# A Winograd-style 3x3 convolution on one core: the weights in transfers of 116 and 12 partitions, one store less finely cut, and two images' loads taken apart

## The chip, the cores and the metric

The kernel runs on one core of a Trainium2 chip. The time is the device time of one execution in microseconds (us). Durations of single steps come from one profiled execution, whose times are counted from the start of its span.

## The reference

A 3x3 convolution with padding 1, 16 images of 64 x 64 pixels with 64 channels in and 128 out, all float32:

```python
batch, c_in, h, w, c_out = 16, 64, 64, 64, 128
x_pad = np.pad(x, ((0, 0), (0, 0), (1, 1), (1, 1)), mode='constant')
output[b, co] += weight[co, ci, kh, kw] * x_pad[b, ci, kh:kh+h, kw:kw+w]   # summed over ci, kh, kw
```

## The kernel before

Two images form a pair: the 64 channels of one lie on partitions 0 to 63, those of the other on 64 to 127. There are eight pairs (0 to 7), and each is worked off in two halves of 32 output rows (the loop that starts at line 218). GpSimd (POOL) forms the sums and differences of input rows that the algorithm needs (`sums`, `diffs`, `outers`, lines 110 to 128; those of the first half are done by VectorE, DVE), ScalarE (ACT) makes a 16-bit copy of some rows (`cast`), TensorE (PE) multiplies by transformed weights (line 170), and ACT and DVE add the results up into output tiles (lines 192 and 247 to 253).

Before that the weights have to be made ready: `w_raw`, 128 rows of 2304 bytes, is loaded (line 59), turned into 16 bits by POOL (line 87) and ACT (line 88), transposed by nine matmuls (line 102), and combined into `Wt` by ACT and DVE (lines 139 to 150). Ahead of its first instruction of line 88 ACT loads its function table, which the compiler places there.

All transfers are issued by SyncE (SP) in the order in which they are written; a wait of one holds up those behind it. SP issues, in this order: the weights; the first pair in two parts (rows 0 to 33 and 34 to 63, called x0a and x0b below); pairs 1 and 2; pairs 3 and 4 in one transfer into the tile `two` (line 81); then the store of pair 0, and from there on stores as pairs are done, with the loads of pairs 5, 6 and 7 among them as their places come free. The pairs 0, 3 and 6 are stored by one transfer of two images (line 207), the others by one for each image (line 216). The second image of pair 5 is an exception: rows 0 to 56 go out in one transfer, and its last seven rows in a transfer of 124 partitions and one of 4:

```python
parts = [(0, CO, 0, H)]
if (p, b2) == FEW[:2]:                 # FEW = 5, 1, 7
    at = H - FEW[2]
    parts = [(0, CO, 0, at), (0, 124, at, H), (124, 4, at, H)]
```

A transfer is cut into packets, one for each contiguous run of a partition (16384 bytes for a whole image of one channel), and these are spread over the rings of up to 16 DMA engines, which work through them in order. The stores are named o0 to o7 here, with a and b for a pair's first and second image where each has its own, and the loads x0a, x0b, x1, x2, x34, x5, x6, x7.

Of the kernel before, what the change touches and what calls it, by code (L numbers as in the profile page):

```python
# [15 lines left out]
def kernel(  # L16
# [12 lines left out]
    nc = tc.nc  # L29
    B, CI, H, W = x.shape  # L30
    CO = weight.shape[0]
# [4 lines left out]
    keep = tc.keep_in_program_order  # L36
    x_rows = x.rearrange("b c h w -> (b c) h w")
    w_flat = weight.rearrange("co ci kh kw -> co (ci kh kw)")
# [10 lines left out]
    X_HOME = [0, 1, 2, ("d", 0), ("d", 1), 2, ("d", 0), ("d", 1)]  # L49
    O_HOME = ["b", (3, 4), (0, 1), "b", (3, 4), (0, 1), "b", (2, 3)]  # L50
    BOTH = (0, 3, 6)
    FEW = 5, 1, 7
    NEXT_LOADS = {(1, 1): 5, (3, 0): 6, (4, 0): 7}

    def home(k, name):
        return slots.tile([128, H, W], F32, tag=f"s{k}", name=name)

    w_raw = const.tile([CO, CI * 9], F32)
    keep(nc.sync.dma_start(w_raw, w_flat))
    xs = {}  # L60

    def load(p, cuts=((0, H),)):
        if X_HOME[p] in range(5):
            xs[p] = home(X_HOME[p], "xs")
        for lo, hi in cuts:
            keep(
                nc.sync.dma_start(
                    xs[p][:, lo:hi, :], x_rows[128 * p : 128 * p + 128, lo:hi, :]
                )
            )  # L70

    two = slots.tile([128, 2, H, W], F32, tag="d", name="two")
# [4 lines left out]
    load(0, ((0, 34), (34, H)))  # L77
    load(1)
    load(2)
    rows = x_rows[128 * 3 : 128 * 5, :, :].rearrange("(g p) h w -> p g h w", g=2)  # L80
    keep(nc.sync.dma_start(two, rows))

    ident = const.tile([128, 128], F16)
    make_identity(nc, ident)
# [113 lines left out]
    def outputs(p):  # L198
        if O_HOME[p] == "b":
            both = slots.tile([128, 2, H, W], F32, tag="b", name="both")  # L200
            return both, [both[:, b2, :, :] for b2 in range(2)]
        return None, [home(k, "ot") for k in O_HOME[p]]

    def store(p, both, ots):
        if p in BOTH:
            pair = out[2 * p : 2 * p + 2, :, :, :].rearrange("b c h w -> c b h w")
            keep(nc.sync.dma_start(pair, both))
            return
        for b2 in range(2):
            parts = [(0, CO, 0, H)]  # L210
            if (p, b2) == FEW[:2]:
                at = H - FEW[2]
                parts = [(0, CO, 0, at), (0, 124, at, H), (124, 4, at, H)]
            for c, n, lo, hi in parts:
                keep(
                    nc.sync.dma_start(
                        out[2 * p + b2, c : c + n, lo:hi, :], ots[b2][c : c + n, lo:hi, :]
                    )
                )

    for n, (p, h) in enumerate(halves):
        if n + 2 < len(halves):
            tr[halves[n + 2]] = transforms(nc.gpsimd, *halves[n + 2])
        if h == 0:
            both, ots = outputs(p)
# [28 lines left out]
        if h == 1:  # L254
            store(p, both, ots)
# [32 lines left out]
```

## Time and profile before

| | us |
|---|---|
| median of 3 runs (lowest to highest) | 127.10 (126.88 to 127.14) |
| the profiled execution's own time | 127.13 |
| its span | 125.4 |
| PE busy / POOL busy / ACT busy / DVE busy | 95.6 / 90.5 / 85.4 / 66.8 |
| bytes moved by DMA, mean rate | 50.78 MB, 405 GB/s over the span |
| last DMA packet of the span | ends at 124.17 |

The profiled execution lies 0.03 us above the median. Of its 127.13 us, 1.73 lie outside the span, and 1.18 inside it after the last packet. The page's busy shares are means over the whole span; its second part cuts the span into 40 slices of 3.1 us, a digit of 9 meaning 90% busy or more.

### The profile page before, as it was taken

To read this page: it belongs to the slowest core of one execution; us is meant where nothing else is said; L and a number is where in the kernel's file an instruction comes from. 1 tells how busy PE (TensorE), PEld (TensorE's weight loads), DVE (VectorE), ACT (ScalarE), POOL (GpSimd) and SP (SyncE) were. 2 spreads that over 40 slices of the span, in tenths; PEclk is the share of its full clock that TensorE was granted. 3 is DMA by queue.
4 is the path that set the end of the run, shared out by engine and by line. 5 is a ranking of instruction groups with operands and counts; after the bars stand their busy time and mean duration, and the time that the engine had idled before them with its cause. 6 is when DMAs were issued, how large, how long until landed. Compare 5 with 4: busy or idle time off the path is not lost.

```text
span 125.4 us, 2343 instructions
## 1 busy us (share of the span) xinstructions
PE 95.6 (76%) x873; PEld 48.9 (39%) x873; DVE 66.8 (53%) x104; ACT 85.4 (68%) x150; POOL 90.5 (72%) x52
## 2 busy tenths in 40 slices
PE   0349999999999999999999999999999960000000
PEld 0223555555455555555555555555555520000000
DVE  0199658393939476574939394765749390000000
ACT  4458598989797988989897979789898930000000
POOL 2209999999999999999999999999999300000000
PEclk9999999999999999999999999999999996555555
DMA  4999999999999999999999999999999999999971
GB/s 132 371 453 423 434 424 439 423 335 418 434 431 429 426 434 418 423 429 434 416 439 424 423 423 423 418 431 434 423 424 423 433 416 443 423 429 444 418 335 47
DMA packets 3827, 50.78 MB, mean 405 GB/s; under 512 B 360, under 2 KB 488, under 8 KB 744
## 3 DMA queue, kind: packets, MB, share of 16 engines
q1 hardware_dynamic: 3816, 50.63, 96.2%
q8 instruction: 7, 0.11, 0.3%
q14 instruction: 4, 0.03, 0.1%
HBM read 17.07 MB, written 33.55 MB: 404 GB/s over the span
## 4 chain that ended last, share of the span: by engine, by line
PE 76%; DMA 2%; DVE 2%; POOL 1%; DVEq 0%; ACT 0%; issue 0%
PE acc L170 75%; DMA w_raw<-in_weight_dram 2%; DVE ss L114 1%; DVE ot L251 1%; POOL w L87 1%; DVEq L283 0%; DVE th L141 0%; DVE Wt L142 0%; PE wp L102 0%; ACT g0h L139 0%; DVEq L142 0%
## 5 line engine op out<-in xcount | busy, mean ns | idle before, releaser
L170 PEld LDWEIGHTS <-Wt 64*128 64x128 f16 x864 | 48.0, 96 | 48.5 <-issue 3.0
L192 ACT COPY ut<-acc 128x512 f32<-128x512 f32 x96 | 48.7, 612 | 4.4 <-PE acc L170 4.4
L170 PE MATMUL acc<-xh,Wt 64*128 64x504 f16 (+3 forms) x384 | 46.2, 372 | 0.0
L170 PE MATMUL acc<-ss,Wt 64*128 64x504 f16 (+1 forms) x192 | 24.8, 392 | 2.3 <-DVE ss L114 2.3
L170 PE MATMUL acc<-ee,Wt 64*128 64x504 f16 (+1 forms) x192 | 26.4, 377 | 0.0
L247 DVE TENSOR_TENSOR ot<-acc,ut 128x512 f32<-128x512 f32 x20 | 12.9, 686 | 20.0 <-ACT ut L192 15.8
L114 POOL TENSOR_TENSOR ss<-xs 128x1024 f16<-128x1024 f32 x7 | 16.6, 2366 | 4.7 <-DMA xs<-in_x_dram 4.7
L127 POOL TENSOR_TENSOR ee<-two 128x1024 f16<-128x1024 f32 x8 | 19.0, 2378 | 0.0
L114 POOL TENSOR_TENSOR ss<-two 128x1024 f16<-128x1024 f32 x8 | 19.0, 2369 | 0.0
L127 POOL TENSOR_TENSOR ee<-xs 128x1024 f16<-128x1024 f32 x7 | 16.6, 2376 | 0.0
L253 ACT COPY ot<-acc 128x512 f32<-128x512 f32 x20 | 10.7, 589 | 5.5 <-PE acc L170 5.5
L170 PE MATMUL acc<-dd,Wt 64*128 64x504 f16 (+1 forms) x96 | 13.9, 392 | 0.0
L247 DVE TENSOR_TENSOR both<-acc,ut 128x512 f32<-128x512 f32 x12 | 7.7, 686 | 11.0 <-ACT ut L192 7.9
L251 DVE TENSOR_TENSOR ot<-ut,acc 128x512 f32<-128x512 f32 x20 | 12.8, 682 | 0.2
L249 DVE TENSOR_TENSOR ot<-acc,ut 128x512 f32<-128x512 f32 x20 | 12.8, 680 | 0.0
L121 POOL TENSOR_TENSOR dd<-two 128x512 f16<-128x512 f32 x8 | 10.3, 1287 | 0.0
L121 POOL TENSOR_TENSOR dd<-xs 128x512 f16<-128x512 f32 x7 | 10.0, 1423 | 0.0
L132 ACT CAST xh<-two 128x1088 f16<-128x1088 f32 x8 | 9.3, 1157 | 0.0
L132 ACT CAST xh<-xs 128x1088 f16<-128x1088 f32 x8 | 9.2, 1145 | 0.0
L253 ACT COPY both<-acc 128x512 f32<-128x512 f32 x12 | 6.4, 589 | 3.5 <-PE acc L170 3.5
L251 DVE TENSOR_TENSOR both<-ut,acc 128x512 f32<-128x512 f32 x12 | 7.7, 683 | 0.1
L249 DVE TENSOR_TENSOR both<-acc,ut 128x512 f32<-128x512 f32 x12 | 7.7, 680 | 0.0
(23 smaller groups left out, 14.9 us busy)
## 6 DMA issues: line engine op xcount, KB each, us to landing
out_dram<-ot SPq DMA_DIRECT2D x9, 2048.0 KB, 18.5
out_dram<-both SPq DMA_DIRECT2D x3, 4096.0 KB, 22.5
xs<-in_x_dram SPq DMA_DIRECT2D x3, 2048.0 KB, 16.2
two<-in_x_dram SPq DMA_DIRECT2D x1, 4096.0 KB, 28.4
two<-in_x_dram SPq DMA_DIRECT2D x2, 2048.0 KB, 23.1
out_dram<-ot SPq DMA_DIRECT2D x1, 1824.0 KB, 24.3
xs<-in_x_dram SPq DMA_DIRECT2D x1, 1088.0 KB, 5.4
xs<-in_x_dram SPq DMA_DIRECT2D x1, 960.0 KB, 7.4
```

What stands on the lines that cost most here:

```text
L87: keep(nc.gpsimd.tensor_copy(w16[:, 0, :], w_raw))
L114: keep(eng.tensor_add(t, v[:, j : j + 16, 0, :], v[:, j : j + 16, 1, :]))
L121: keep(eng.tensor_sub(t, v[:, j : j + RB, 1, :], v[:, j : j + RB, 0, :]))
L127: keep(eng.tensor_sub(t, xs[p][:, r - 1 : r + 15, :], xs[p][:, r + 1 : r + 17, :]))
L132: keep(nc.scalar.copy(t, xs[p][:, C_ROW[h] : C_ROW[h] + 17, :]))
L170: nc.tensor.matmul(tiles[b2][:, lo:hi, c_lo:c_hi], Wt[p0 : p0 + 64, wi, kw, :], src[p0 : p0 + 64, first : last + 1 : step, c_lo + kw - 1 : ...
L192: keep(nc.scalar.copy(ut, tiles[b2]))
L247: keep(nc.vector.tensor_add(ov[b2][:, jg : jg + RB, 1, :], pg2[b2], ug[b2]))
L249: keep(nc.vector.tensor_add(ov[b2][:, jf : jf + RB, 0, :], pf1[b2], uy[b2]))
L251: keep(nc.vector.tensor_sub(ov[b2][:, jf : jf + RB, 1, :], ux[b2], pf2[b2]))
L253: keep(nc.scalar.copy(ov[b2][:, jg : jg + RB, 0, :], pg1[b2]))
```

## The change

Three edits. The weights come in two transfers, of partitions 0 to 115 and 116 to 127. Pairs 3 and 4 are loaded by a transfer each. The second image of pair 5 is stored by one transfer of 128 partitions, as the other single images are. The number of transfers stays at 24.

```diff
-    FEW = 5, 1, 7
+    FEW = 116
...
-    keep(nc.sync.dma_start(w_raw, w_flat))
+    for c in (slice(0, FEW), slice(FEW, CO)):
+        keep(nc.sync.dma_start(w_raw[c, :], w_flat[c, :]))
...
-    rows = x_rows[128 * 3 : 128 * 5, :, :].rearrange("(g p) h w -> p g h w", g=2)
-    keep(nc.sync.dma_start(two, rows))
+    load(3)
+    load(4)
...
         for b2 in range(2):
-            parts = [(0, CO, 0, H)]
-            if (p, b2) == FEW[:2]:
-                at = H - FEW[2]
-                parts = [(0, CO, 0, at), (0, 124, at, H), (124, 4, at, H)]
-            for c, n, lo, hi in parts:
-                keep(
-                    nc.sync.dma_start(
-                        out[2 * p + b2, c : c + n, lo:hi, :], ots[b2][c : c + n, lo:hi, :]
-                    )
-                )
+            keep(nc.sync.dma_start(out[2 * p + b2, :, :, :], ots[b2]))
```

## The prediction, made before the result was known

> **What bounds the kernel now.** The page's slices come first: they show which resource is never idle.
>
> ```profile
> PE   0349999999999999999999999999999960000000
> ...
> DMA  4999999999999999999999999999999999999971
> GB/s 132 371 453 423 434 424 439 423 335 418 434 431 429 426 434 418 423 429 434 416 439 424 423 423 423 418 431 434 423 424 423 433 416 443 423 429 444 418 335 47
> ```
>
> The DMA engines are full from the second slice to the 38th of 40; PE stops in the 33rd. The windows view of the end says the same:
>
> ```profile
> 28.40:100.00 71.60, 71.60 (x676) 36.78 (x672) 45.51 (x74) 63.69 (x114) 69.88 (x36) 1.00 1.01 426
> 100.00:119.40 19.40, 2.41 (x24) 0.98 (x18) 3.68 (x6) 1.44 (x3) 0.00 (x0) 0.62 1.01 430
> 119.40:124.20 4.80, 0.00 (x0) 0.00 (x0) 0.00 (x0) 0.00 (x0) 0.00 (x0) 0.50 0.51 218
> ```
>
> The share before the last figure is the DMA's: full to 119.4, half in the last 4.8 us, where rings finish one after the other. So the end is set by the last of 16 rings, and the page's chain, which ends in PE, misleads: PE only hands over stores, and those wait behind others.
>
> The trace also keeps every DMA packet with start, duration and bytes, without its ring. In steady state a packet starts 2 to 4 ns before the one ahead of it ends, so I strung the packets into 16 rings by fitting starts to ends and sizes to the issue order (in the first 3 us the fit is ambiguous). A 16384-byte packet takes 611 ns, 607 from start to start. Rings end between 120.18 and 124.17. Four facts matter. (1) The 128 packets of 1792 bytes (124 + 4 partitions) lie on four rings, 32 on each; these end at 122.60, 122.91, 123.20 and 123.38. (2) One ring, the slow ring, has stores of 644 ns in the median against 611; it ends at 124.07 and is none of the four. (3) The last, the late ring, ends at 124.17; it lost some 0.6 us to an instruction packet of 16 KB at 21.3 us and then 2.8 us to slow loads (the last two packets of x34, the last three of x6); it is none of the four either. (4) The other ten end at 122.62 or sooner.
>
> The start comes next: the chain in order of time, then SP and ACT in the timeline.
>
> ```profile
> 0.74 2.95 DMA w_raw<-in_weight_dram
> ...
> 3.74 0.67 POOL w L87
> ...
> 8.00 94.44 PE acc L170 x864
> ```
>
> ```profile
> 0.74 0.38 SPq L59 DMA_DIRECT2D w_raw<-in_weight_dram  x1
> 1.18 0.42 SPq L67 DMA_DIRECT2D xs<-in_x_dram  x1
> 34.14 0.36 SPq L216 DMA_DIRECT2D out_dram<-ot  x1
> 80.76 0.33 SPq L216 DMA_DIRECT2D out_dram<-ot  x1
> 81.15 1.67 SPq L216 DMA_DIRECT2D out_dram<-ot  x2
> 0.73 1.28 ACT L88 ACT_TABLE_LOAD   x1 [0.73 <-PEq L272]
> 3.71 0.67 ACT L88 CAST w<-w_raw 128x576 f16<-128x576 f32 x1 [1.70 <-DMA w_raw<-in_weight_dram]
> ```
>
> PE runs 94.44 us without a pause, so what it loses at the start it never regains. The fifth SP row is the pair of 124 and 4 partitions: 0.78 and 0.83 us of issue by the trace, where whole transfers of 128 partitions that wait for nothing take 0.33 to 0.45.
>
> **The store of pair 5.** The other twelve rings, slow and late one among them, get 16384 bytes a row instead of 14592: 8 rows x 66 ns (607 less 541) = +0.53 us; on the slow ring, 5% slower, +0.56. The four rings lose 32 packets of 70 ns (2.24 us) and gain 0.53: -1.71. Two transfers and their 1.6 us of issue go; that costs or saves nothing, as the next store waits until 92.3 us for its data.
>
> **The weights on the rings.** From fact (1), 124 went to four rings of 31 and 4 to four of 1, so 116 goes to four rings with 29 packets. For 12 no row shows whether three or one a ring. (By the Trainium skill, "DMA: Bandwidth & Descriptors", section "Why a DMA increments its semaphore by 16 and not by 1", the count is the largest divisor up to 16, so twelve rings; no run here shows it.) At 90 ns a packet after the first, the four rings get 21 or more on top of their 8, +2.0 us, against -1.71 from the store: +0.3, ending at 123.7. They stay behind the slow and the late ring.
>
> **The start of the loads.** Twelve rings lose 7 or 8 weight packets; the weights occupy them from 1.74-2.30 to 2.8-3.3, then x0a starts at 2.79-3.29. But x0a is now issued third. Two bounds. If the new issues take what the old one took (0.38), x0a is issued at 1.60; with the 1.01 to 1.56 that the weights needed from issue to first packet it starts at 2.6-3.16: -0.15. If they cost what 124 and 4 partitions cost (0.78 and 0.83, and two gaps of 0.05), x0a is issued at 2.45 and starts at 3.46-4.0: +0.7. Below the first bound a gain needs the slow first x0a packets (0.34 us of excess a ring) to vanish too. I take +0.7: these rows are the nearest, also transfers over few rings, and their waits (transfers ended 10 us before) can't fill the time. (The Trainium skill, same page, "Issuing engines are not separate DMA queues", says the time to initiate a DMA is usually small relative to the DMA itself; the pair's 1.67 us contradicts it here. By it the sum would come out as in the first rival.)
>
> **The weights' way to PE.** The four rings finish 29 packets, with the first one's 0.3 us, at about 4.8, and the 12 partitions at 4.9, against 3.3. In the built program ACT's table load, which waited for nothing, now waits for the 12 partitions. So 1.28 us that lay beside the transfer comes behind it: ACT's copy ends near 5.3 + 1.28 + 0.67 = 7.3 instead of 4.4, and PE starts about 2.9 us late. Every store is handed over 2.9 us late. Cover: the tightest is o1a, issued at 34.14 and reached by the first ring at 37.92, 3.8 us of which an issue needs up to 1.56. It becomes ready at 38.0-38.6; most rings, moved by +0.7, want it at 38.6 or later, the slow ring (38.55 before) at 39.2. So nothing is lost, or some tenths on rings with over 1.5 us to spare at the end. o0, issued at 23.24 and wanted at 28.2, has more. Last data: o7a moves from 103.18 to 106.1, wanted at 110.4.
>
> **Pairs 3 and 4 apart.** The same 16 packets a ring, pair 3 sooner; no reader waited (POOL's only wait for data is 4.7 us at the start). One completion write more, 6 ns. All rings' last two packets of x34 are slow (0.63 us together, at 26 to 28 us; 1.7 on the late ring). I leave that where it is; bounds -0.6 if it belonged to the two-image form, +1 if four rings pay as the late ring did, which puts them at 124.7, still not last.
>
> **Sum.** Slow ring 124.07 + 0.56 + 0.7 = 125.3; late ring 124.17 + 0.53 + 0.7 = 125.4. That is +1.2 us on 127.13, or on the median 127.1: 128.3.
>
> **Rivals.** First: the issues stay short, x0a starts 0.15 early, so +0.4: 127.5. For it: in 'two' a whole transfer in the opening burst took 0.71 us, so long issues may come from a crowd and not from few rings. Against: 80 us has no such crowd, with 0.33 right before.
>
> Second, the other side: the weights' packets leave the slow ring and x0a really comes sooner. If x0a is issued at 1.60, starts on that ring 1.13 later as its weights did, and takes 8 x 325 ns without the excess, it ends at 5.33 instead of 6.26: -0.93 + 0.56 = -0.37, 126.7. It decides as soon as the slow ring ends x0a before 5.70, which asks for an x0a issue by 1.97, and for a late ring that loses less to its slow loads. Against it: the 0.78 and 0.83.
>
> Third: stores starve. If PE starts over 4.1 us late, o1a comes too late for the slow ring; at 5 us late it costs 0.9 more, 129.2. Against it: the 2.9 has the measured table load in it already.
>
> **How the numbers follow.** Forecast 0.62 (128.3, own range 127.9 to 128.8); short issues 0.18 (127.3 to 127.8, nearly half of it within 0.2%, 0.25 us, about what a measurement of this kernel can tell from no change); other side 0.13; starving 0.07. Hence faster 0.13, same 0.10 (0.08, and 0.02 from a shorter x34 end under long issues), slower 0.77. The range leaves out the other side and starving: 127.2 to 128.8.
>
> **What would show it.** SP's second and third issue rows (near 0.8 us each, x0a at about 2.4); ACT's table load after the weights at about 5.3; PE from about 10.9; no row of the DMA share below 1.0 between 28 and 100; rings ending at about 125.3. An x0a issue at 1.6 makes the start wrong; an empty DMA stretch near 38 makes the cover wrong; a last ring that is one of the four makes the balance wrong.

## The result, and the profile after

The changed kernel takes 129.81 us in the median of six runs (129.54 to 130.46) beside 127.12 for the kernel before (126.88 to 127.20): a ratio of 1.0225, interval 1.0204 to 1.0245. It is slower, by 2.7 us, and lies above the forecast's range (127.2 to 128.8). The profiled execution took 129.54 with a span of 127.7. Here and below, a kernel's executions that took over 1.5% longer than its fastest are left out of the ratios, but not out of the medians.

Line numbers move by one or more (59 becomes 60, 67 becomes 68, 170 becomes 171). The same slices of the page of the changed kernel:

```profile
PE   0012999999999999999999999999999993000000
...
DMA  2899999999999999999999999999999999999991
GB/s 34 257 414 445 411 426 462 421 411 416 457 426 398 431 439 313 354 359 431 449 416 416 421 416 447 431 421 418 436 431 426 421 436 431 426 426 436 436 400 62
```

Two things stand out against before. The first two slices moved 34 and 257 GB/s (132 and 371 before), and slices 16 to 18, from 48 to 57 us, moved 313, 354 and 359 though the DMA row has its 9 there. The single dip of before, 335 in slice 9 (25 to 28 us), is gone.

The start, in the timeline of SP, ACT and POOL and in the chain in order of time (start, duration):

```profile
0.74 0.37 SPq L60 DMA_DIRECT2D w_raw<-in_weight_dram  x1
1.53 0.36 SPq L68 DMA_DIRECT2D xs<-in_x_dram  x1
27.35 0.40 SPq L208 DMA_DIRECT2D out_dram<-both  x1
6.96 1.28 ACT L89 ACT_TABLE_LOAD   x1 [6.96 <-DMA w_raw<-in_weight_dram]
7.01 0.67 POOL L88 CAST w<-w_raw 128x576 f16<-128x576 f32 x1 [5.71 <-DMA w_raw<-in_weight_dram]
```

```profile
1.17 5.71 DMA w_raw<-in_weight_dram
12.54 2.75 PE acc L171 x12
15.29 91.27 PE acc L171 x852
```

The issues are short, x0a goes out at 1.53. But the weights are there only at 7.0 instead of 3.7, the table load stands behind them, PE starts at 12.54 instead of 8.00, and the first store is issued at 27.35 instead of 23.24.

The windows view puts numbers on the stretches; columns are length, busy time and count of PE, weight load, DVE, ACT and POOL, PE clock, DMA share, GB/s. First the kernel before, then the changed one, for 2 to 4, 4 to 6.5, 25.5 to 28.5 and 47 to 56 us:

```profile
2.00:4.00 2.00, 0.00 (x0) 0.00 (x0) 0.00 (x0) 0.30 (x2) 0.26 (x1) 1.00 1.03 328
4.00:6.50 2.50, 1.15 (x9) 0.92 (x9) 0.80 (x2) 1.25 (x3) 0.41 (x1) 1.00 0.96 393
25.50:28.50 3.00, 3.00 (x31) 1.53 (x28) 3.00 (x6) 2.34 (x5) 3.00 (x2) 1.00 1.03 339
...
47.00:56.00 9.00, 9.00 (x90) 4.62 (x86) 5.87 (x10) 7.91 (x15) 9.00 (x6) 1.00 1.01 426
```

```profile
2.00:4.00 2.00, 0.00 (x0) 0.00 (x0) 0.00 (x0) 0.00 (x0) 0.00 (x0) 1.00 0.54 101
4.00:6.50 2.50, 0.00 (x0) 0.00 (x0) 0.00 (x0) 0.00 (x0) 0.00 (x0) 1.00 0.96 299
25.50:28.50 3.00, 3.00 (x32) 1.37 (x28) 1.73 (x3) 2.78 (x6) 3.00 (x3) 1.00 1.00 421
...
47.00:56.00 9.00, 9.00 (x88) 4.10 (x84) 6.95 (x12) 7.69 (x14) 9.00 (x5) 1.00 1.02 353
```

The figure before the last is the share of the DMA engines that is busy. From 2 to 4 us rings stand empty (share 0.54). From 4 to 6.5 and from 47 to 56 they are full and yet move less, because single packets take longer. The stretch from 25.5 to 28.5 has become fast.

Strung into 16 rings as in the prediction, the packets show at which stage the mean ring falls behind. The table has the time at which the rings finish a transfer, as a mean over the rings. "Excess" is what 16384-byte packets take beyond 611 ns, in us and as a mean over the rings:

| end of | before | after | behind | what happened in the stage |
|---|---|---|---|---|
| x1 | 13.20 | 15.02 | 1.82 | the start |
| the loads x3, x4 | 28.62 | 29.78 | 1.16 | before: 0.77 of excess, after: 0.08 |
| o1a | 43.40 | 44.63 | 1.23 | nothing |
| o1b | 48.29 | 50.07 | 1.78 | before: 0.02 of excess, after: 0.55 |
| x5 | 53.27 | 56.28 | 3.01 | before: 0.06 of excess, after: 1.21 |
| o7b, the last | 122.14 | 125.04 | 2.90 | nothing more |

So the mean ring loses 1.8 us at the start and 1.75 around x5, and gains 0.7 at the end of the loads. The last ring moved less, from 124.17 to 126.36.

### The profile page after: what moved, and what is told of

It reads as the page before. It is cut to its first block, busy times and chain, and to the rows that moved or that the text cites. A ratio compares the mean times of both kernels' runs of the same rounds, so it can differ in the third digit from the quotient of the medians.

```text
span 127.7 us, 2345 instructions
## 1 busy us (share of the span) xinstructions
PE 95.1 (75%) x873; PEld 43.5 (34%) x873; DVE 67.2 (53%) x104; ACT 85.3 (67%) x150; POOL 91.6 (72%) x52
## 4 chain that ended last, share of the span: by engine, by line
PE 74%; DMA 4%; DVE 2%; ACT 2%; DVEq 0%; issue 0%; SPq 0%; ACTq 0%
PE acc L171 74%; DMA w_raw<-in_weight_dram 4%; ACT L89 1%; DVE ss L115 1%; ACT w L89 1%; DVE ot L243 1%; DVEq L275 0%; DVE th L142 0%; DVE Wt L143 0%; PE wp L103 0%; ACT g0h L140 0%; SPq L60 0%; DVEq L143 0%; ACTq L89 0%
## 5 line engine op out<-in xcount | busy, mean ns | idle before, releaser
L171 PEld LDWEIGHTS <-Wt 64*128 64x128 f16 x864 | 42.6, 95 | 53.5 <-issue 2.9
L171 PE MATMUL acc<-xh,Wt 64*128 64x504 f16 (+3 forms) x384 | 45.7, 370 | 0.0
L115 POOL TENSOR_TENSOR ss<-xs 128x1024 f16<-128x1024 f32 x7 | 17.2, 2459 | 4.1 <-DMA xs<-in_x_dram 4.1
L128 POOL TENSOR_TENSOR ee<-xs 128x1024 f16<-128x1024 f32 x7 | 17.7, 2529 | 0.0
L171 PE MATMUL acc<-dd,Wt 64*128 64x504 f16 (+1 forms) x96 | 13.0, 377 | 0.0
L239 DVE TENSOR_TENSOR both<-acc,ut 128x512 f32<-128x512 f32 x12 | 7.7, 686 | 10.0 <-ACT ut L193 9.9
L122 POOL TENSOR_TENSOR dd<-xs 128x512 f16<-128x512 f32 x7 | 9.5, 1352 | 0.0
L103 PE MATMUL wp<-ident,w 128*128 128x128 f16 x9 | 1.1, 312 | 9.1 <-ACT w L89 9.1
## 6 DMA issues: line engine op xcount, KB each, us to landing
xs<-in_x_dram SPq DMA_DIRECT2D x3, 2048.0 KB, 14.7
```

The costliest lines, as they stand in the source:

```text
L103: keep(nc.tensor.matmul(wp[:, k * CO : k * CO + CO], w16[:, :, 3 * kh + k :: 9], ident))
L115: keep(eng.tensor_add(t, v[:, j : j + 16, 0, :], v[:, j : j + 16, 1, :]))
L122: keep(eng.tensor_sub(t, v[:, j : j + RB, 1, :], v[:, j : j + RB, 0, :]))
L128: keep(eng.tensor_sub(t, xs[p][:, r - 1 : r + 15, :], xs[p][:, r + 1 : r + 17, :]))
L171: nc.tensor.matmul(tiles[b2][:, lo:hi, c_lo:c_hi], Wt[p0 : p0 + 64, wi, kw, :], src[p0 : p0 + 64, first : last + 1 : step, c_lo + kw - 1 : ...
L239: keep(nc.vector.tensor_add(ov[b2][:, jg : jg + RB, 1, :], pg2[b2], ug[b2]))
```

## The experiments

All are edits of one of the two kernels. Times are medians, ratios are against the kernel before on the same chip, whose median was 126.9 to 127.1 in every group. Where rings, excess, first stores and PE's start are given, they come from the one profiled execution of that run.

**The three edits, each alone.** The weights in 116 and 12 partitions, nothing else:

```diff
-    keep(nc.sync.dma_start(w_raw, w_flat))
+    for c in (slice(0, 116), slice(116, CO)):
+        keep(nc.sync.dma_start(w_raw[c, :], w_flat[c, :]))
```

> The kernel before with the weights' split (116 and 12) alone. Theory 'start': the split alone brings the late landing of the weights (6.4 to 7.0 us instead of 3.7), ACT's table load behind it and the slow first loads, so the rings begin x1 about 1.8 us later in the mean and the whole takes 2.2 to 3.0 us more than before (129.3 to 130.1). Its slow packets then lie not at the end of x34 but at the second store of pair 1 and at x5, as in the changed kernel. Rival 'sum of edits': the split alone costs only its start, 1.2 to 1.8 us less what moves, and the slow x5 comes from loading pairs 3 and 4 apart: 128.0 to 128.9, with x5 at full speed (under 0.2 us of excess a ring).

Measured: 130.91 us, ratio 1.0333 (1.0307 to 1.0359), above the band of the first theory by 0.8. PE starts at 12.29; the rings finish x1 at 15.81 or sooner, 1.7 us late in the mean; x34 ends with 0.07 us of excess a ring, o1b and x5 have 0.60 and 1.28. The split alone makes the whole picture of the changed kernel, the slow x5 too. It is 1.1 us slower than the changed kernel. For this the trace shows two things: four rings carry the weights' 29 packets and the 32 extra packets of pair 5's store, and three of these four end last, at 126.6 to 127.6; and the rings stand empty for some 0.5 us ahead of o1a, against 0.06 in the changed kernel.

Pairs 3 and 4 by a transfer each, nothing else (lines 81 and 82 become `load(3)` and `load(4)`):

> The kernel before with pairs 3 and 4 loaded by a transfer each, nothing else. Theory 'start': this edit does nothing: the same packets in the same time, 127.1 within 0.3, and the last two packets before the first store stay slow (0.6 to 0.8 us a ring). Rival 'sum of edits': the slow packets at the end of the loads belong to the form with two images and vanish, 126.4 to 126.7, or slow packets appear at x5 instead (128 or more).

Measured: 127.10 us, ratio 1.0013 (0.9995 to 1.0030): no change, with the slow end of the loads still there (0.91 us a ring on x4). The edit does nothing that can be measured, as the prediction had it.

The second image of pair 5 in one transfer, nothing else (the last hunk of the diff):

> The kernel before with the second image of pair 5 stored by one transfer, nothing else. By the sum of the prediction twelve rings get 0.53 us more (the slow ring 0.56) and four lose 1.7: the slow or the late ring ends the run at about 124.7 instead of 124.2, so 127.6 to 127.7. Rival: the last ring is set by chance stalls and not by this balance, 127.1 within 0.2.

Measured: 127.66 us, ratio 1.0056 (1.0042 to 1.0070), the last rings ending at 124.50 and 124.27. This is the +0.53 of the prediction's balance, 0.7 by the medians. The three edits alone give 3.9 + 0.1 + 0.7 = 4.7 us, together 2.7: the whole store takes from the four rings what the weights' split put on them.

**What of the split costs.** First, the cut moved so that both transfers lie on 16 rings:

```diff
-    FEW = 116
+    FEW = 112
```

> The changed kernel with the weights cut into 112 and 16 partitions instead of 116 and 12, so that both transfers use 16 rings (7 packets and 1) while ACT's table load still waits for the second one. Theory 'start by concentration': with 29 packets on four rings gone the weights land near 4.0, PE starts some 1.5 us late (the table load alone) and rings begin x1 within 0.4 us of before: 127.2 to 127.9. Rival 'two transfers as such': issuing one transfer more and the table load make the loss whatever the cut, 129 or more.

Measured: 128.19 us, ratio 1.0109 (1.0091 to 1.0127), above the first theory's band by 0.3 and far under the rival's. The weights land at 3.8, PE starts at 9.43, 1.43 us late, and the timeline shows why: the table load still waits for the second transfer.

```profile
3.83 1.28 ACT L89 ACT_TABLE_LOAD   x1 [3.83 <-DMA w_raw<-in_weight_dram]
```

The rings finish x1 0.6 us late in the mean, not 0.4 (three of them at 14.7 to 15.0, where the latest of before is 13.5), and x4 is slow (0.97) as in the kernel before while x5 is fast (0.09). So of the start's 1.8 us some 1.2 come from the 29 packets on four rings.

Second, 120 and 8 partitions, which spread evenly, but over fewer than 16 rings:

> The changed kernel with the weights cut into 120 and 8 partitions, which lie evenly (8 rows a ring on fifteen rings, one a ring on eight) but on fewer than 16. Theory 'concentration': the start is as with 112 and 16 (weights land near 3.9, x1 within 0.6 us of before in the mean), 127.8 to 128.4. Rival 'fewer than 16 rings costs by itself': the first loads start late and slow as in the changed kernel, 129 or more.

Measured: 129.43 us, ratio 1.0166 (1.0102 to 1.0230), single runs from 127.81 to 129.69. By its number the rival would be right, by the trace it is not: the weights land at 3.85 and the rings finish x1 0.5 us late in the mean, as with 112. But PE starts at 10.02, as it waits for x0a, which lands at 8.72 because a few rings are late; the first store is issued at 25.96; and o1b and x5 have 0.56 and 1.05 of excess, while x4 has 0.21. What costs is not the rings' mean start but what the later first store brings with it.

Third, the changed kernel with the table load out of the weights' way:

```diff
+    idle = const.tile([128, 8], F32)
+    keep(nc.vector.memset(idle, 0.0))
+    for _ in range(1):
+        keep(nc.scalar.copy(idle, idle))
     w16 = const.tile([CO, 2, CI * 9], F16)
```

> The changed kernel with a copy of 8 elements on ACT ahead of the weights' copy (its data set by DVE), so that ACT's table load no longer waits for the 12 partitions. The rings' start is as in the changed kernel (x1 about 1.8 us late in the mean). Theory 'handed over late': PE starts near 11.3 instead of 12.5, the first store is issued near 26.1 and is queued before the loads end, so the slow end of the loads (0.7 us a ring) comes back and the slow second store of pair 1 and x5 (1.75 us a ring) go: 128.3 to 129.0. Rival 'split of the weights as such': slow x5 stays, 129.5 to 130.0.

Measured: 129.06 us, ratio 1.0165 (1.0138 to 1.0193), between the two bands. PE starts at 11.21, the first store goes out at 26.45, and x5 stays slow (0.32 and 1.35). The 1.3 us that PE gained bring some 0.7; the first store is still too late for the old picture, so the expectation had the turning point wrong.

**Is it the lateness, or the split as such?** The kernel before, its transfers untouched, with ten copies on ACT ahead of the weights' copy, and then with eight:

```diff
+    idle = const.tile([128, 512], F32)
+    keep(nc.vector.memset(idle, 0.0))
+    for _ in range(10):
+        keep(nc.scalar.copy(idle, idle))
     w16 = const.tile([CO, 2, CI * 9], F16)
```

> The kernel before with ten copies of 512 elements on ACT ahead of its copy of the weights, which leave the transfers as they are and make PE start about 4.5 us late. Theory 'handed over late': the rings start as before, the slow end of x34 goes, the second store of pair 1 and x5 turn slow (1.5 to 1.9 us a ring), and o1a, issued near 38.6 where the rings want it at 37.3, leaves them empty for about 2: 129 to 130.5. Rival 'split of the weights as such': x5 stays fast and only the empty stretch costs, 127.1 to 128.5.

Measured: 129.95 us, ratio 1.0234 (1.0199 to 1.0268). First store issued at 27.58; x34 ends without excess (0.04), o1b and x5 have 0.63 and 1.12, and rings stand empty for 0.67 us before or in o0 and 0.89 in o1a.

> The same with eight copies, PE about 3.2 us late, so that the first store is issued near 26.5, 1.7 us before the rings reach it. Theory 'handed over late': between the two, the slow end of x34 goes and either the slow x5 is there (128 to 129) or neither is (126.4 to 126.9). Rival: 127.1 within 0.3, as PE's start has no part in the end.

Measured: 129.56 us, ratio 1.0209 (1.0183 to 1.0235). PE's start came out at 12.68, as late as with ten (12.75), and the picture is the same: first store at 27.69, excess 0.05 in x34, 0.62 and 1.15 in o1b and x5. The point in between was missed, but both runs say that a late PE with the old transfers is enough for the slow x5.

Then the first store held back, with PE on time (8.01) and the next stores only 0.7 us later than before (34.88 instead of 34.14). SP waits for it in a small store out of pair 1's result:

```diff
...
+    spot = spare.tile([128, 64], F32)
...
         for b2 in range(2):
             keep(nc.vector.tensor_add(ov[b2][:, jg : jg + RB, 1, :], pg2[b2], ug[b2]))
+        if n == 2:
+            keep(nc.sync.dma_start(spot, ots[0][:, 1, :]))
+            store(0, *first)
...
-        if h == 1:
+        if n == 1:
+            first = both, ots
+        elif h == 1:
             store(p, both, ots)
```

> The kernel before with the first store alone held back: SP issues it behind a small transfer of 128 x 256 bytes out of a row of pair 1's result, which is there near 25.9 us, so that o0 is issued near 26.4 instead of 23.2; all else (PE's start, o1a at 34.1) stays as it was. Theory 'late first store': the time at which the first store is queued decides where the slow packets lie; x34 ends fast (0.7 us a ring gained), and the second store of pair 1 and x5 turn slow (1.5 to 1.9 us a ring): 128.0 to 129.0. Rival 'late everything': the slow x5 needs the other stores late too, or rings that ran empty; x34 ends fast, x5 stays fast: 125.6 to 126.8.

Measured: 128.10 us, ratio 1.0056 (1.0019 to 1.0093), where the first theory had it. SP's rows of the small store, the first store and the next ones, and the windows for 25.5 to 28.5 and 47 to 56 us:

```profile
26.63 0.34 SPq L251 DMA_DIRECT2D spot<-ot  x1
27.01 0.43 SPq L209 DMA_DIRECT2D out_dram<-both  x1
34.88 1.77 SPq L218 DMA_DIRECT2D out_dram<-ot  x2
```

```profile
25.50:28.50 3.00, 3.00 (x32) 1.53 (x30) 2.59 (x5) 2.56 (x5) 3.00 (x2) 1.00 0.88 365
...
47.00:56.00 9.00, 9.00 (x88) 4.52 (x86) 5.14 (x9) 8.34 (x15) 9.00 (x6) 1.00 1.00 348
```

348 GB/s from 47 to 56, with full rings, as in the changed kernel (353). One store issued at 27.01 instead of 23.24 is enough: x34 loses its excess (0.04), o1b and x5 get 0.74 and 1.20. The small store that the edit adds is hardly the cause: in a run further down, a store of this size, queued early, leaves both places as they were before. Over the runs the first store's issue sorts the kernels:

| kernel | first store issued | rings reach it (median) | excess at the end of the loads | excess in o1b and x5 |
|---|---|---|---|---|
| before | 23.24 | 28.45 | 0.77 | 0.08 |
| 112 and 16 | 24.25 | 28.99 | 0.97 | 0.11 |
| 120 and 8 | 25.96 | 28.11 | 0.21 | 1.60 |
| table load early | 26.45 | 29.18 | 0.05 | 1.68 |
| first store held | 27.01 | 28.04 | 0.04 | 1.94 |
| changed | 27.35 | 29.58 | 0.06 | 1.76 |
| weights' split alone | 28.10 | 29.53 | 0.07 | 1.89 |

With four us or more between issue and need the loads' last two packets are slow and x5 fast; with under three it is the other way, and that way costs 0.7 to 1.1 us more a ring. Each row is one execution, and no row lies between 2.7 and 4.7 us, so where it turns isn't known.

Two attempts at where the slow end of the loads comes from put a small store (128 x 256 bytes of zeros to spare memory) early, behind x0b on SP's queue, and ahead of everything from ACT:

> The kernel before with a small store (128 x 256 bytes of zeros to spare memory) put into SP's queue behind the first pair's loads. Theory 'first change from loads to stores': the slow packets are paid once, where the first store follows loads on a ring; they move from the end of x34 to the end of x0b, where packets are smaller, and x34 ends fast: 126.0 to 126.8. Rival: the slow end of x34 has to do with the large store behind it, stays at 0.7 to 0.8 us a ring, and the time is 127.0 to 127.3.

Measured: 127.98 us, ratio 1.0024 (0.9985 to 1.0063), so no change is shown; in its profile x34 ends as slow as before (0.83 us a ring), and o1b and x5 together have 0.07. The first theory falls: the slow packets are not paid once by any first store.

> The same small store issued by ACT before anything else, while the rings are still empty. Theory 'first store is slow by itself': x34 ends fast, 126.0 to 126.8. Rival: no change of x34, 126.9 to 127.3.

Measured: 127.56 us, ratio 1.0029 (0.9988 to 1.0070), no change shown. The one profiled execution took 129.69 us and had its first store only at 25.16, so it can't be set beside the others, and the run settles nothing.

**Why the start is slow.** The changed kernel with the weights' two transfers behind x0a and x0b, so that nothing there waits for an issue:

> The changed kernel with the first pair's two loads issued ahead of the weights, so that the weights' 29 packets lie on four rings behind x0b while the other twelve have x1 behind it, and every issue is done some 5 us before the rings need it. The whole gets slower, as PE starts later; the question is x1 on the twelve rings beside the weights (from about 8 to 11 us). Theory 'late descriptors': x0a's packets were late and slow in the changed kernel because they were issued behind the weights' with the rings empty; here x1's packets on the twelve rings start without a gap and take 611 ns. Rival 'shared reading': the weights on four rings slow the reading of the others; x1's packets beside them take 800 ns or more.

A single run took 138.55 us, as PE starts at 21.58. Its windows for 4.5 to 7.5 (x0a and x0b alone), 8 to 12 (weights on four rings, x1 on twelve) and 13 to 20 us:

```profile
4.50:7.50 3.00, 0.00 (x0) 0.00 (x0) 0.00 (x0) 0.00 (x0) 0.00 (x0) 1.00 0.99 416
8.00:12.00 4.00, 0.00 (x0) 0.00 (x0) 0.00 (x0) 0.00 (x0) 0.00 (x0) 1.00 1.04 247
13.00:20.00 7.00, 1.15 (x9) 1.02 (x10) 2.84 (x3) 4.51 (x7) 6.07 (x4) 1.00 1.00 426
```

All rings are full, and the rate falls from 416 to 247 GB/s while the weights run. x1's packets take 990 to 1170 ns, as means of half a microsecond, instead of 611, the weights' own 150 to 180 instead of 93, and x1's recover as soon as the weights are through. So packets on twelve rings get slow beside the weights on the other four even where nothing waits for an issue. Two things stay open. Whether the four rings or the small packets (2304 bytes) do it isn't separated, as no run has such packets on 16 rings beside long ones. And the run says nothing on the empty rings from 2 to 4 us of the changed kernel, where x0a's first packets come late.

## Why the prediction was wrong, point by point

**What bounds the kernel** held: the last ring sets the end, with the rings full and PE done 20 us before.

**The store of pair 5** held: +0.53 on twelve rings, and 0.7 measured with that edit alone.

**The weights on the rings** held in the count: 29 packets on four rings, and the page's 368 packets under 512 bytes, one completion write for each ring of a transfer, are 22 x 16 + 4 + 12, so the 12 partitions did go to twelve rings. It also held in that the four aren't last, though it was close: by the fit they end at 124.9 to 126.06, the last ring at 126.36. Their extra 2.0 us were 2.6 at the start of x0b, against the mean ring of before.

**The start of the loads** was the first step that failed. The rows taken as nearest, 0.78 and 0.83 us for 124 and 4 partitions, do not carry over: the two issues take 0.37 and 0.31 us, and x0a is issued at 1.53, which is the lower bound. So the Trainium skill's sentence that the issue is usually small ("DMA: Bandwidth & Descriptors", section "Issuing engines are not separate DMA queues") holds here, and the row against it was misread; what made those two long stays open. The loss was there all the same, and twice as large: the twelve rings start x0b at 7.1 to 7.7 instead of 5.7 to 6.3, 1.4 late instead of 0.7. About half of it is a late first packet: x0a starts on these rings at 3.06 to 4.27, where before it was 2.79 to 3.29. That is near the 3.46 to 4.0 of the prediction by luck, since the long issues that it was worked out from did not happen; from issue to first packet it took 1.5 to 2.7 us instead of 1.01 to 1.56, and why isn't shown. The other half is slow packets: from 3 to 6.5 us x0a's took 420 to 1010 ns, as means of half a microsecond, where 328 is their time without excess; the weights ran until 5.99. In all that is 0.9 us a ring, where before has 0.4. The start itself has a share in it: in the last run above, where x0a goes first with no weights beside it, it has 0.7, but is at 329 ns 1.3 us after its first packet, and not only after 3.5. The sum priced each ring by its own packets and had no term for the others' packets getting slow beside them. The late first packets and the slow ones also undid the first rival, which had the short issues right and stayed at 127.5.

**The weights' way to PE** had the table load right, 1.28 us behind the 12 partitions. The landing was mis-sized: 5.3 forecast, 7.0 measured, so PE is 4.5 us late and not 2.9. The last of the weights' packets ended at 5.99 and not at 4.9, and from there to the landing it took 0.9 us, where it was 0.4 before.

**The cover of the stores** was the second step that failed. It asked only whether rings run empty, and there it came out nearly right, though PE was 4.5 us late where it had reckoned with 2.9: o1a loses 0.06 us a ring to gaps, since the rings were late too. But the first store, 4.1 us later, turned the slow end of the loads (-0.7) into a slow o1b and x5 (+1.75). The prediction had seen the slow end of x34 and left it "where it is"; it depends on when the store behind it is queued. Holding that store back, with PE on time, shows it.

**Pairs 3 and 4 apart** held: 1.0013.

**The sum** was +1.2 on the last ring; measured were +2.2 there in the profile, made of about +1.8 for the start, +1.05 for the slow packets and +0.5 for the store, less some 1.2 that is left over. The likely place of that is the late ring of before, which had 1.7 us of excess in the last two packets of x34 that the changed kernel's last ring does not have; this is a balance, not a test. The third rival came nearest (stores handed over late, 129.2) with the wrong mechanism: not empty rings, slow packets.

## What to carry to other kernels

A small transfer whose partition count put it on four of sixteen rings cost more here than its own packets, while the other rings read: look at the rate of the stretch, not only at the rings' shares. Where the DMA engines bound a kernel, as here, a late store can cost time with every ring full, so compare GB/s stretch by stretch, not only the DMA row. And look in the built program for waits that an edit hangs onto instructions it doesn't name: splitting one load into two put ACT's 1.28 us table load behind it.

## What the runs showed of the hardware that was not expected

Beside 2304-byte loads on four rings the loads on the others got slow: 247 GB/s instead of 416, with all rings busy. One of the rings has stores of 640 to 660 ns instead of 611 in nearly every run, its loads being as fast as those of the others. Around changes between loads and stores packets get slow, in one of two places by the time of the first store's issue: 0.8 to 1.0 us a ring at the end of the first loads, or 1.6 to 1.9 in the store and load that follow later. What in the memory or the engines does this wasn't found; the small early store on SP's queue only rules out that any first store pays it.
